# Hybrid encoder trunk on one core: phases in another order, the first 20 loads in a set order, two output projections 512 columns wide, transposes emitted ahead of attention

## The chip, the core and the metric

The kernel runs on one core of a Trainium2 chip. A core has TensorE (PE: matmuls and transposes, its weight loads shown as PEld), VectorE (DVE), ScalarE (ACT), GpSimd (POOL) and SyncE (SP, which here issues every DMA from one queue). Each engine takes its instructions in the order of the program and waits for the others by semaphores. The metric is the device time of one execution in microseconds, as the median of several runs.

## The reference

Two layers over a prompt `p` (1024 tokens) and a sample `s` (512 tokens) of width 1024, with the same weights. Each layer normalizes, projects once, runs three branches (even layer: gated short convolution, sliding-window attention, attention over 256 memory rows; odd layer: axial-rotary attention, differential attention, memory attention), gates with SiLU and projects back.

```python
def trunk(x, mem, norm_g, w_in, w_out, mem_norm_g, w_mem_kv, mem_qk_g, conv_w, swa_qk_g,
          swa_sink, ax_qk_g, diff_qk_g, diff_lambda, diff_subln_g):
...
    for l in range(DEPTH):
        h = rms_norm(x, norm_g[l])
        u = h @ w_in[l]
        mkv = rms_norm(mem, mem_norm_g[l]) @ w_mem_kv[l]
...
        if l % 2 == 0:
            y1 = short_conv(gb, gc, hc, conv_w[e])
            y2 = window_attention(q, k, heads(v, SWA_KV_HEADS), swa_sink[e])
        else:
            y1 = dense_gqa(q, k, heads(v, AX_KV_HEADS))
            y2 = diff_attention(dq, dk, heads(dv, DIFF_HEADS), diff_lambda[o], diff_subln_g[o], l)
        ym = memory_attention(mq, mk, mv)
        y = jnp.concatenate([y1, y2, ym], axis=-1)
        x = x + (y * jax.nn.silu(z)) @ w_out[l]
    return x
```

## The kernel before

**Arithmetic.** Matmuls run on fp32r numbers. So that no precision is lost, an operand is split in two: `hi` is its rounding (ACT casts), `lo` the rest (DVE or POOL subtracts, `split`, L198). A product takes three matmuls: hi x hi, hi x lo, lo x hi (L322 to L324, L336 to L338). Attention takes two (L596, L597).

**Phases.** `STEPS` is a list of phases, each a call of `step`: `in g l chunks` projects 512 or 1024 tokens onto 256-column chunks of `w_in` (`in_proj`, matmul tiles `pa`, `pb0`, `pb1`); `swa`, `ax`, `diff`, `mem` are the attentions (scores `s`, exponentials `e`, transposes `pT`, outputs `o`); `load` and `loady` fetch h or y from DRAM and split them (`alo`, `ahi`); `out g l half` is an output projection of 512 tokens (`out_proj`, tile `po`), which adds x (`xr`) and stores; `norm` normalizes rows for the next layer (transposes `hT`, products with the gain `hg`, `ht`). g is `p` or `s`, l the layer.

**An output projection** goes through four chunks of 256 columns. For each it loads five pieces of weights (`load_w`: `wraw`, 256 KB, split in `whi` and `wlo`), and for four tiles of 128 tokens it adds up 10 steps of 128 rows in one PSUM half bank, three matmuls of 128x256 each, so each piece is used by four tiles in turn. Two tiles share a bank, one VectorE addition empties it (L935).

**What sets the order.** The program is written phase by phase; a scheduler then orders each engine's instructions by priority and readiness. Attention phases are `urgent` (high priority), so their instructions are woven into the projections that are written after them. Small background steps (`BG`: norms, rope tables) and the pending transposes of projected heads (`TAIL`, `STACK`: `stT` with its source `raw`) are put in at `between` and `flush`, in the middle of a projection's matmuls. `ring` gives tiles out of a set number of buffers (`BUF_TABLE`: three `wraw`, seven `whi` and `wlo`, three `xh` for x, PSUM tags `s` 2, `t` 2, `d` 2, `x` 1, `o` 1 banks), and `in_order` keeps the first writes of a ring's tiles in the order in which they were asked for.

**The start.** Norm steps of the four memory tiles (`x`, `hT`, `hg`, `h0`, `h1`) come first, then the rope tables (`rope_table`, a POOL multiplication of 128x1024, L170), constants, the memory projection `mem_kv` (tile `pm`) and the norm of the first half of the prompt.

## Time and profile before

| | |
|---|---|
| time, median of 3 runs (lowest to highest) | 2108.88 us (2107.57 to 2109.26) |
| the profiled execution's own time | 2099.39 us |
| its span | 2097.6 us |
| mean granted TensorE clock over the span | 0.997 |
| busy: PE, DVE, ACT, POOL | 97%, 74%, 53%, 46% |

The span runs from the program's first instruction to its last. A stretch of the span is given by its start and end in us from the start. A matmul's duration is from its start to its modelled end; the next may start long before that end, so PE's throughput is read from the distance between starts, or from a count in a stretch. In a list of instructions, the bracket behind a row is the time for which the engine stood idle just ahead of it, and what ended that.

### The profile page before, as it was taken

What the parts mean: (1) busy time and instruction counts of PE and PEld (TensorE: products, weight loads), DVE (VectorE), ACT (ScalarE), POOL (GpSimd) and SP (SyncE); (2) the same over time, 40 slices, a digit from 0 to 9 for tenths busy, and PEclk for the clock granted to TensorE, in tenths of its full rate; (3) what the DMA queues carried; (4) which work ended last, traced back from release to release, by engine and by line L of the source; (5) the groups of instructions that cost most, each with busy time, mean ns of one, the idle gap of its engine ahead of it and who ended that gap; (6) DMA issues with size and microseconds to landing.
All of it is one profiled execution on the core that took longest, in us unless ns stands there. A gap on an engine that the chain in (4) does not pass through costs nothing.

```text
span 2097.6 us, 40483 instructions
## 1 busy us (share of the span) xinstructions
PE 2040.2 (97%) x14056; PEld 1885.0 (90%) x14056; DVE 1552.4 (74%) x3340; ACT 1115.9 (53%) x2634; POOL 969.9 (46%) x994
## 2 busy tenths in 40 slices
...
GB/s 236 206 241 197 228 106 91 118 101 217 238 236 224 209 93 82 104 154 128 82 151 154 226 164 178 151 199 213 169 218 199 160 191 193 157 235 225 233 159 106
DMA packets 323420, 365.79 MB, mean 174 GB/s; under 512 B 28048, under 2 KB 229520, under 8 KB 323216
## 3 DMA queue, kind: packets, MB, share of 16 engines
...
q14 instruction: 93, 0.76, 0.1%
...
## 4 chain that ended last, share of the span: by engine, by line
PE 75%; DMA 7%; DVE 7%; issue 3%; POOL 2%; ACT 1%; SPq 1%; DVEq 0%; POOLq 0%; ACTq 0%
PE pb L338 8%; PE pb L336 8%; PE pb L337 8%; PE pa L323 5%; PE pa L324 5%; PE pa L322 5%; PE po L322 4%; PE po L323 4%; PE po L324 4%; PE s L596 4%; PE s L597 4%; PE o L754 3%; PE pT L750 3%; PE o L685 1%; PE pT L683 1%
## 5 line engine op out<-in xcount | busy, mean ns | idle before, releaser
L200 POOL TENSOR_TENSOR wlo<-wraw,whi 128x512 fp32r<-128x512 f32 x182 | 249.0, 1370 | 329.1 <-ACT whi L199 309.9
L695 ACT ACTIVATE e<-s,nm 128x512 f32<-128x512 f32 (+1 forms) x416 | 265.1, 640 | 221.2 <-DVE nm L693 167.4
L199 ACT CAST whi<-wraw 128x512 fp32r<-128x512 f32 x388 | 236.9, 622 | 238.8 <-PE po L324 84.6
L604 DVE TENSOR_TENSOR ptlo<-pT,pthi 128x512 fp32r<-128x512 f32 x352 | 237.3, 683 | 41.6 <-ACT pthi L603 40.0
L693 DVE TENSOR_REDUCE nm<-s 128x1 f32<-128x512 f32 (+1 forms) x368 | 249.0, 682 | 25.7 <-PE s L597 24.4
L603 ACT CAST pthi<-pT 128x512 fp32r<-128x512 f32 x352 | 199.1, 588 | 114.6 <-PE pT L683 56.6
L322 PE MATMUL po<-whi,ahi 128*128 128x256 f32 x896 | 254.0, 284 | 0.4 <-DVE xr L935 0.4
L324 PE MATMUL po<-whi,alo 128*128 128x256 f32 x896 | 253.1, 284 | 1.3 <-DVE alo L200 1.3
L323 PE MATMUL po<-wlo,ahi 128*128 128x256 f32 x896 | 254.2, 284 | 0.0
L200 DVE TENSOR_TENSOR wlo<-wraw,whi 128x512 fp32r<-128x512 f32 x206 | 170.8, 830 | 95.3 <-ACT whi L199 92.5
L236 POOL TENSOR_TENSOR rs<-ss,mhalf 128x8 f32<-128x8 f32 (+2 forms) x108 | 141.1, 1307 | 174.4 <-DVE ss L232 125.2
L322 PE MATMUL pa<-whi,ahi 128*128 128x256 f32 x768 | 220.2, 287 | 0.5 <-ACT raw L394 0.4
L324 PE MATMUL pa<-whi,alo 128*128 128x256 f32 x768 | 219.2, 286 | 0.5 <-DVE alo L200 0.5
L323 PE MATMUL pa<-wlo,ahi 128*128 128x256 f32 x768 | 219.2, 285 | 0.0
L596 PE MATMUL s<-k,qhh 128*128 128x512 f32 (+2 forms) x512 | 190.1, 376 | 10.5 <-ACT e L695 9.6
L597 PE MATMUL s<-k,qll 128*128 128x512 f32 (+2 forms) x512 | 182.9, 363 | 2.8 <-DMA qll<-st_p1mq 1.6
L324 PEld LDWEIGHTS po<-whi,alo 128*128 128x128 f32 x896 | 171.0, 191 | 3.2 <-DVE alo L200 1.7
L322 PEld LDWEIGHTS po<-whi,ahi 128*128 128x128 f32 x896 | 171.1, 191 | 1.9 <-DVE xr L935 0.6
L323 PEld LDWEIGHTS po<-wlo,ahi 128*128 128x128 f32 x896 | 171.1, 191 | 1.2
L336 PE MATMUL pb<-h,whi 128*128 128x512 f32 x432 | 170.9, 396 | 0.0
L338 PE MATMUL pb<-h,wlo 128*128 128x512 f32 x432 | 170.7, 395 | 0.0
L337 PE MATMUL pb<-h,whi 128*128 128x512 f32 x432 | 170.6, 395 | 0.0
(170 smaller groups left out, 6022.7 us busy)
## 6 DMA issues: line engine op xcount, KB each, us to landing
wraw<-in_w_in_dram SPq DMA_DIRECT2D x252, 256.0 KB, 3.3
wraw<-in_w_out_dram SPq DMA_DIRECT2D x120, 256.0 KB, 3.2
...
zg_p<-z SPq DMA_DIRECT2D x32, 256.0 KB, 2.7
...
```

The source lines that it names most:

```text
L200: lo_eng.tensor_tensor(out=out_lo, in0=src, in1=f32(out_hi), op=ALU.subtract)
L322: nc.tensor.matmul(out=out, lhsT=h, rhs=wh, start=(k == 0), stop=False)
L323: nc.tensor.matmul(out=out, lhsT=h, rhs=wl, start=False, stop=False)
L324: nc.tensor.matmul(out=out, lhsT=l_, rhs=wh, start=False, stop=(k == n - 1))
L336: nc.tensor.matmul(out=out, lhsT=wh, rhs=h, start=(k == 0), stop=False)
L337: nc.tensor.matmul(out=out, lhsT=wh, rhs=l_, start=False, stop=False)
L338: nc.tensor.matmul(out=out, lhsT=wl, rhs=h, start=False, stop=(k == n - 1))
L596: nc.tensor.matmul(out=out, lhsT=q2[0], rhs=k, start=True, stop=False)
L597: nc.tensor.matmul(out=out, lhsT=q2[1], rhs=k, start=False, stop=True)
L604: nc.vector.tensor_tensor(out=lo, in0=ps, in1=f32(hi), op=ALU.subtract)
L693: nc.vector.tensor_reduce(out=nm, in_=s, axis=AXL.X, op=ALU.max, negate=True)
L695: nc.scalar.activation(out=e[:, j, :], in_=s[:, j, :], func=ACTF.Exp, bias=nm[:, j:j + 1], accum_out=su[:, j:j + 1],)
```

## The change

1. `STEPS`: the phases stand in another order at nine places (chunks moved between `in` steps, `diff p 1 0` ahead of `diff p 0 0`, `mem p 1 0` ahead of `diff p 2 0`, `mem s 1` behind `out p 1 0`, and others).
2. `load_w` now takes single steps of 128 rows, 512 columns of them: `w_out` lies in DRAM as 10 x 128 rows x 512 columns per half, and a narrow projection reads 256-column parts of it, two steps to a piece.
3. `out p 0 0` and `out s 1 0` become `outk`: `out_proj_k` goes through two chunks of 512 columns, holds four PSUM banks (two of tag `d`, two of `t`), one for each tile of 128 tokens, and for each of the 10 steps runs all four tiles, three matmuls of 128x512 each. Each of the four additions takes a whole bank.
4. At the start, 20 transposes of the identity; the first memory weights are asked for ahead of the rope tables and constants, which move behind the second x of the prompt; `ORDER` chains the first 20 loads (and the tiles that they write) in the order of the text.
5. `step` calls `flush` ahead of every attention phase, and `loady` calls `gate_now`, so pending transposes and gates are written ahead of it.

```diff
@@ -37,16 +37,16 @@
 CHUNKS = [L0_CHUNKS, L1_CHUNKS]
 STEPS = [
     "in p 0 kv0+q0+z4", "swa p 0", "in p 0 q1+z6+mq0", "swa p 1", "in p 0 z8", "mem p 0",
-    "in p 0 gch0+gbz0+gch1+gbz1+gch2+gbz2", "loady p 0 0 0 4", "in p 0 gch3+gbz3", "loady p 0 0 4 5",
-    "loady p 0 1", "out p 0 0", "norm p 0", "out p 0 1", "norm p 1", "load m", "load p 1 01", "memkv m",
-    "in p 1 kv0+q0+z0", "ax p 0", "in p 1 q1+z2+dk0+dv0", "ax p 1", "in p 1 dq0+z4", "diff p 0 1", "diff p 0 0",
-    "diff p 1 0", "in p 1 dq1+dv1", "in p 1 z6 0", "in p 1 dk1", "in p 1 mq0+z8 0", "load s 0 0",
-    "in s 0 kv0+q0+z4", "swa s 0", "in s 0 q1+z6", "swa s 1", "in s 0 mq0+z8", "mem s 0", "diff p 1 1",
-    "in s 0 gch0+gbz0+gch1+gbz1+gch2+gbz2+gch3", "load p 1 1", "in s 0 gbz3", "loady s 0 0 0 4", "in p 1 z6 1",
-    "diff p 2 0", "diff p 3 0", "mem p 1 0", "out s 0 0", "norm s", "in p 1 mq0+z8 1", "diff p 2 1", "diff p 3 1",
-    "in s 1 dv0", "mem p 1 1", "in s 1 kv0+q0+z0", "ax s 0", "in s 1 q1+dk0+z2+dq0", "ax s 1", "in s 1 z4",
-    "diff s 0", "diff s 1", "loady p 1 0", "in s 1 dk1+dq1+mq0+dv1+z8+z6", "diff s 2", "diff s 3", "mem s 1",
-    "loady p 1 1", "out p 1 0", "loady s 1 0 0 4", "out p 1 1", "out s 1 0",
+    "in p 0 gch0+gbz0+gch1+gbz1+gch2+gbz2+gch3", "loady p 0 0 0 4", "in p 0 gbz3", "loady p 0 0 4 5",
+    "loady p 0 1", "outk p 0 0", "norm p 0", "out p 0 1", "norm p 1", "load m", "load p 1 01", "memkv m",
+    "in p 1 kv0+q0+z0", "ax p 0", "in p 1 q1+dk0+dv0+z2", "ax p 1", "in p 1 dq0+z4", "diff p 1 0",
+    "in p 1 dq1+dv1", "diff p 0 0", "diff p 0 1", "in p 1 z6 0", "in p 1 dk1", "in p 1 mq0 0", "load s 0 0",
+    "in p 1 z8 0", "in s 0 kv0+q0+z4+q1", "swa s 0", "in s 0 z6", "swa s 1", "in s 0 mq0+z8", "mem s 0",
+    "diff p 1 1", "in s 0 gch0+gbz0+gch1+gbz1+gch2+gbz2+gch3", "load p 1 1", "in s 0 gbz3", "loady s 0 0 0 4",
+    "in p 1 z6 1", "mem p 1 0", "diff p 2 0", "diff p 3 0", "out s 0 0", "norm s", "in p 1 mq0+z8 1", "in s 1 dv0",
+    "diff p 2 1", "diff p 3 1", "in s 1 q0+kv0", "mem p 1 1", "in s 1 z0", "ax s 0", "in s 1 q1+dk0+z2+dq0",
+    "ax s 1", "in s 1 z4", "diff s 0", "diff s 1", "loady p 1 0", "in s 1 dk1+dq1+mq0+dv1+z8+z6", "diff s 2",
+    "diff s 3", "loady p 1 1", "out p 1 0", "loady s 1 0 0 4", "mem s 1", "out p 1 1", "outk s 1 0",
 ]
 BUF_TABLE = {
     "act": 16, "whi": 7, "wlo": 7, "wraw": 3, "xh": 3, "stk": 4, "bw": 5, "tb": 2, "sm": 12, "nm": 8, "sx": 6, "su": 12, "sk": 4, "s4": 2,
@@ -139,12 +139,21 @@
     lam_init = 0.8 - 0.6 * math.exp(-0.3 * 1)
     CW = const.tile([128, 4, 3], F32, name="convw_half")
 
+    ORDER = []
+
+    def loaded(t):
+
+        if len(ORDER) < 20:
+            ORDER.append(t)
+        return t
+
     def load_constants():
+        for t in (wmask, nsink, convw, gsub):
+            loaded(t)
         nc.sync.dma_start(out=wmask, in_=a["wmask"].rearrange("s p j -> p s j"))
         nc.sync.dma_start(out=nsink, in_=a["swa_sink"][0].partition_broadcast(128))
         nc.vector.tensor_scalar(out=nsink, in0=nsink, scalar1=-1.0, scalar2=None, op0=ALU.mult)
         nc.sync.dma_start(out=convw, in_=a["conv_w"])
-        nc.sync.dma_start(out=mg, in_=a["mem_qk_g"].partition_broadcast(128))
         nc.sync.dma_start(out=gsub, in_=a["diff_subln_g"].rearrange("o p -> p o"))
         nc.vector.tensor_scalar(out=gsub, in0=gsub, scalar1=0.5 * (1.0 - lam_init), scalar2=None, op0=ALU.mult)
         lv = tabt(4 * HD, "lv").rearrange("p (k d) -> p k d", k=4)
@@ -214,16 +223,20 @@
         return g
 
     @first
-    def load_w(src, pairs):
+    def load_w(src, ks, wide=False):
+
+
         hi, lo = [], []
-        for kp in pairs:
-            lo_ = ring(sb, [128, 2, 256], F32R, "wlo", "wlo")
-            h = ring(sb, [128, 2, 256], F32R, "whi", "whi")
-            raw = ring(sb, [128, 2, 256], F32, "wraw", "wraw")
-            dma(out=raw, in_=src[kp].rearrange("p (k n) -> p k n", k=2))
-            split(h, lo_, raw, nc.vector if kp % 2 == 0 else nc.gpsimd)
-            hi.append(h)
-            lo.append(lo_)
+        for k in ks:
+            l_ = ring(sb, [128, 512], F32R, "wlo", "wlo")
+            h = ring(sb, [128, 512], F32R, "whi", "whi")
+            raw = loaded(ring(sb, [128, 512], F32, "wraw", "wraw"))
+            dma(out=raw if len(src.shape) == 3 else raw.rearrange("p (i n) -> p i n", i=2), in_=src[k])
+            split(h, l_, raw, nc.vector if k % 2 == 0 else nc.gpsimd)
+            for i in range(1 if wide else 2):
+                sl = slice(0, 512) if wide else slice(256 * i, 256 * i + 256)
+                hi.append(h[:, sl])
+                lo.append(l_[:, sl])
         return hi, lo
 
     def rstd(out, ss, mul, add):
...
@@ -922,7 +935,9 @@
         for ci in range(4):
             if ahead and ci == 3:
                 ahead()
-            w = load_w(a["w_out"][l, ci], Y_ORDER[g, l])
+            w = load_w(
+                a["w_out"][l, ci // 2][:, :, ci % 2 * 256:ci % 2 * 256 + 256].rearrange("(k i) p n -> k p i n", i=2), Y_ORDER[g, l]
+            )
             for tp in range(2):
                 ps = ring(psum, [128, 2, 256], F32, "d", "po")
                 for t in range(2):
@@ -935,6 +950,37 @@
                 nc.vector.tensor_tensor(out=xr, in0=ps, in1=xr, op=ALU.add)
                 dma(out=dst[rows, cols].rearrange("(t p) n -> p t n", p=128), in_=xr)
 
+    def out_proj_k(g, l, hf, ys):
+
+
+        src = a[f"x_{g}"] if l == 0 else S[g, "x1"]
+        dst = S[g, "x1"] if l == 0 else a[f"out_{g}"]
+        order = [2 * kp + i for kp in Y_ORDER[g, l] for i in range(2)]
+        for ci in range(2):
+            cols = slice(ci * 512, (ci + 1) * 512)
+            rows = [slice(hf * 512 + t * 128, hf * 512 + (t + 1) * 128) for t in range(4)]
+            ps = [ring(psum, [128, 512], F32, "d", "pk") for _ in range(2)]
+            ps += [ring(psum, [128, 512], F32, "t", "pk", "A") for _ in range(2)]
+            xr = []
+            for n, k in enumerate(order):
+                (wh,), (wl,) = load_w(a["w_out"][l, ci], [k], True)
+                hi, lo = ys[n // 2]
+                for t in range(4):
+                    sl = slice(t * 128, (t + 1) * 128)
+                    h, l_ = hi[:, n % 2, sl], lo[:, n % 2, sl]
+                    nc.tensor.matmul(out=ps[t], lhsT=h, rhs=wh, start=(n == 0), stop=False)
+                    nc.tensor.matmul(out=ps[t], lhsT=h, rhs=wl, start=False, stop=False)
+                    nc.tensor.matmul(out=ps[t], lhsT=l_, rhs=wh, start=False, stop=(n == 9))
+                if n < 9:
+                    between(0)
+                if n >= 5 and n < 9:
+                    x = bw("xr")
+                    dma(out=x, in_=src[rows[n - 5], cols])
+                    xr.append(x)
+            for t in range(4):
+                nc.vector.tensor_tensor(out=xr[t], in0=ps[t], in1=xr[t], op=ALU.add)
+                dma(out=dst[rows[t], cols], in_=xr[t])
+
 
     nxt = {}
 
@@ -948,17 +994,23 @@
 
     hm, hp = new_h(), [new_h(), new_h()]
     gains = const.tile([128, 4, KT], F32, name="gains")
-    dma(out=gains, in_=a["gains"])
     g0, g1, gm0, gm1 = (gains[:, i, :] for i in range(4))
+    warm = ring(psum, [128, 4, 128], F32, "x", "warm")
+    for n in range(20):
+        nc.tensor.transpose(warm[:, n % 4, :], ident, ident)
     BG.extend(norm_steps(mem_rows(), put_act(hm, gm0), "s"))
-    bg(12)
+    bg()
+    dma(out=loaded(gains), in_=a["gains"])
+    w0 = load_w(a["w_mem_kv"][0, 0], range(2))
+    bg()
+    w1 = load_w(a["w_mem_kv"][0, 0], range(2, 4))
+    bg(10)
+    dma(out=loaded(mg), in_=a["mem_qk_g"].partition_broadcast(128))
     BG.extend(norm_steps(rows_of(a["x_p"]), put_act(hp[0], g0), "s"))
-    bg(3)
-    rope_table("swa_k", "e")
-    rope_table("swa_q", "e")
-    load_constants()
-    mem_kv(0, hm)
-    bg(12)
+    BG[2:2] = [lambda: rope_table("swa_k", "e")]
+    BG[4:4] = [lambda: rope_table("swa_q", "e"), load_constants]
+    mem_kv(0, hm, w0=tuple(x + y for x, y in zip(w0, w1)))
+    bg(len(BG))
     BG.extend(norm_steps(rows_of(a["x_p"], 1), put_act(hp[1], g0), "s"))
     BG.extend(norm_steps(rows_of(a["x_s"]), put_dram(S["s", 0, "h"], 0, g0)))
     BG.extend(norm_steps(mem_rows(), put_dram(S["m", 1, "h"], 0, gm1)))
@@ -972,14 +1024,16 @@
         flush()
 
     def step(op, g, *x):
+        if op in ("swa", "ax", "diff", "mem"):
+            flush()
         if op == "in":
             l = int(x[0])
             ids = [CHUNKS[l].index((c.rstrip("0123456789"), int(c.lstrip("abcdefghijklmnopqrstuvwxyz")))) for c in x[1].split("+")]
             in_proj(g, l, H[g, l], ids, hfs=[int(h) for h in x[2]] if len(x) > 2 else None)
         elif op == "swa":
-            swa(g, int(x[0]))
+            swa(g, *map(int, x))
         elif op == "ax":
-            ax(g, int(x[0]))
+            ax(g, *map(int, x))
         elif op == "diff":
             diff(g, int(x[0]), int(x[1]) if len(x) > 1 else None)
         elif op == "mem":
...
                 H[g, l] = [load_half(g, l, hf) if hf in hfs else None for hf in range(GROUPS[g] // 512)]
         elif op == "loady":
+            gate_now()
             settle()
             l, hf = int(x[0]), int(x[1])
             part = slice(int(x[2]), int(x[3])) if len(x) > 2 else slice(0, 5)
             YS.setdefault((g, l, hf), []).extend(load_y(g, l, hf, part))
@@ -1070,7 +1126,7 @@
     out["mem_s"] = f["mem_sample"][0]
     out["w_in"] = np.stack([np.stack([pieces(f["w_in"][l], cols(l, *c)) for c in CHUNKS[l]]) for l in range(2)])
     out["w_out"] = np.stack(
-        [np.stack([pieces(f["w_out"][l], np.arange(256 * c, 256 * c + 256)) for c in range(4)]) for l in range(2)])
+        [f["w_out"][l].reshape(10, 128, 2, 512).transpose(2, 0, 1, 3) for l in range(2)])
     out["w_mem_kv"] = np.stack(
         [np.stack([pieces(f["w_mem_kv"][l], np.arange(256 * c, 256 * c + 256)) for c in range(2)]) for l in range(2)])
     out["conv_w"] = f["conv_w"][0].reshape(3, 4, 128).transpose(2, 1, 0)

```

Three places show what this does to the engines' own orders.

SP, the first DMAs of the program. `x` are tiles of 128 tokens to be normalized, `wraw` weights, `cs` and `g` a rope table's parts. Before:

```order
L119 DMA x<-in_mem_p_dram 128x1024 x2
L119 DMA x<-in_mem_s_dram 128x1024
L119 DMA gains<-in_gains_dram 128x32
L167 DMA g_300<-in_rope_g_dram 128x128
L169 DMA cs<-in_rope_dram 128x1024
L167 DMA g_307<-in_rope_g_dram 128x128
L169 DMA cs<-in_rope_dram 128x1024
L143 DMA wmask<-in_wmask_dram 128x2x128
L144 DMA nsink<-in_swa_sink_dram 128x8
L146 DMA convw<-in_conv_w_dram 128x12
L147 DMA mg<-in_mem_qk_g_dram 128x256
L148 DMA gsub<-in_diff_subln_g_dram 128x1
```

And with the change:

```order
L119 DMA x<-in_mem_p_dram 128x1024
L157 DMA gsub<-in_diff_subln_g_dram 128x1
L119 DMA gains<-in_gains_dram 128x32
L119 DMA wraw<-in_w_mem_kv_dram 128x512 x2
L119 DMA x<-in_mem_p_dram 128x1024
L119 DMA wraw<-in_w_mem_kv_dram 128x512 x2
L119 DMA x<-in_mem_s_dram 128x1024
L119 DMA wraw<-in_w_mem_kv_dram 128x512
L119 DMA x<-in_mem_s_dram 128x1024
L119 DMA mg<-in_mem_qk_g_dram 128x256
L119 DMA wraw<-in_w_mem_kv_dram 128x512 x2
```

The weights of the memory projection, behind all of the rows shown before, now alternate with the x; rope tables and the other constants come later.

PE, inside `out p 0 0`, with buffer numbers; the first operand's halves are `whi`, `wlo`, the second's `ahi`, `alo`. Before:

```order
L322 MATMUL po_6157<-whi_6063,ahi_5713 128x256
L323 MATMUL po_6157<-wlo_6062,ahi_5713 128x256
L324 MATMUL po_6157<-whi_6063,alo_5712 128x256
L322 MATMUL po_6157<-whi_6063,ahi_5713 128x256
L323 MATMUL po_6157<-wlo_6062,ahi_5713 128x256
L324 MATMUL po_6157<-whi_6063,alo_5712 128x256
L322 MATMUL po_6157<-whi_6069,ahi_5720 128x256
```

And with the change:

```order
L971 MATMUL pk_6083<-whi_6238,ahi_6042 128x512
L972 MATMUL pk_6083<-wlo_6237,ahi_6042 128x512
L973 MATMUL pk_6083<-whi_6238,alo_6041 128x512
L971 MATMUL pk_6084<-whi_6238,ahi_6042 128x512
L972 MATMUL pk_6084<-wlo_6237,ahi_6042 128x512
L973 MATMUL pk_6084<-whi_6238,alo_6041 128x512
L971 MATMUL pk_6085<-whi_6238,ahi_6042 128x512
L972 MATMUL pk_6085<-wlo_6237,ahi_6042 128x512
L973 MATMUL pk_6085<-whi_6238,alo_6041 128x512
L971 MATMUL pk_6086<-whi_6238,ahi_6042 128x512
```

One piece of weights now serves four accumulators in a row, at twice the columns, where before one accumulator went through all pieces.

VectorE, at the end of `out p 0 0` and the beginning of `out p 0 1`. `alo` is the split of y (`alo_6041` to `alo_6055` before, `alo_6048` to `alo_6076` after belong to the second half of y), `xr` an addition that empties a bank, `wlo` a weight's split, `ss`, `x` and `ht` the norm. Before:

```order
L935 TENSOR_TENSOR xr_6698<-po_6637,xr_6698 128x512
L259 TENSOR_SCALAR x_6702<-x_6702,rs_6707 128x1024
L232 TENSOR_SCALAR ss_6714<-ss_6714 128x1
L259 TENSOR_SCALAR x_6711<-x_6711,rs_6716 128x1024
L200 TENSOR_TENSOR alo_6048<-alo_6048,ahi_6049 128x512 x2
L200 TENSOR_TENSOR wlo_6922<-wraw_6924,whi_6923 128x512
L277 TENSOR_TENSOR ht_6774<-hT_6769,gains_139 128x512
L200 TENSOR_TENSOR alo_6055<-alo_6055,ahi_6056 128x512
L277 TENSOR_TENSOR ht_6812<-hT_6807,gains_139 128x512
L200 TENSOR_TENSOR alo_6055<-alo_6055,ahi_6056 128x512
L277 TENSOR_TENSOR ht_6894<-hT_6889,gains_139 128x512
```

And with the change:

```order
L209 TENSOR_TENSOR alo_6069<-alo_6069,ahi_6070 128x512 x2
L209 TENSOR_TENSOR wlo_6510<-wraw_6512,whi_6511 128x512
L209 TENSOR_TENSOR alo_6076<-alo_6076,ahi_6077 128x512 x2
L209 TENSOR_TENSOR wlo_6522<-wraw_6524,whi_6523 128x512
L209 TENSOR_TENSOR alo_7323<-alo_7323,ahi_7324 128x512 x2
L209 TENSOR_TENSOR wlo_6528<-wraw_6530,whi_6529 128x512
L209 TENSOR_TENSOR alo_7330<-alo_7330,ahi_7331 128x512
L981 TENSOR_TENSOR xr_6395<-pk_6283,xr_6395 128x512
L209 TENSOR_TENSOR alo_7330<-alo_7330,ahi_7331 128x512
L981 TENSOR_TENSOR xr_6415<-pk_6284,xr_6415 128x512
L209 TENSOR_TENSOR wlo_6703<-wraw_6705,whi_6704 128x512
L981 TENSOR_TENSOR xr_6435<-pk_6285,xr_6435 128x512
```

The last splits of y moved from behind the last addition to ahead of the last four; two splits of h for the memory (`alo_7323`, `alo_7330`) stand there now.

## Rows read from the trace of the kernel before

**Rows 1.** The page, part 1: busy us (share of the span), instructions.
```profile
PE 2040.2 (97%) x14056; PEld 1885.0 (90%) x14056; DVE 1552.4 (74%) x3340; ACT 1115.9 (53%) x2634; POOL 969.9 (46%) x994
```
**Rows 2.** Stretches: length, busy us of each engine, clock, DMA share, GB/s.
```profile
0.00:26.00 26.00, 12.00 (x51) 10.61 (x52) 18.65 (x28) 11.62 (x23) 15.19 (x19) 1.00 0.79 263
1200.00:1600.00 400.00, 390.56 (x2455) 349.02 (x2454) 337.08 (x777) 235.84 (x591) 177.31 (x182) 0.99 0.63 189
```
**Rows 3.** Chain that ended last: start us, us on the chain, what.
```profile
500.12 0.12 PE po L323
...
111.42 0.23 PE pb L336
```
**Rows 4.** Stretches inside `out p 0 0` and inside an `in p 0` phase.
```profile
500.00:540.00 40.00, 40.00 (x336) 40.00 (x335) 12.70 (x19) 10.98 (x19) 7.34 (x7) 1.00 0.63 200
476.00:492.00 16.00, 16.00 (x72) 13.24 (x71) 9.17 (x16) 5.47 (x10) 1.30 (x1) 1.00 0.63 201
```
**Rows 5.** Groups by shape (count | busy us, mean ns), 493 to 551, last 1440 to 1680.
```profile
L200 DVE TENSOR_TENSOR wlo<-wraw,whi 128x512 fp32r<-128x512 f32 x13 | 8.9, 690 | 18.1 <-ACT whi L199 17.9
...
L199 ACT CAST whi<-wraw 128x512 fp32r<-128x512 f32 x19 | 11.6, 619 | 32.7 <-PE po L324 21.9 <-DMA wraw<-in_w_out_dram 10.2
...
L200 DVE TENSOR_TENSOR wlo<-wraw,whi 128x512 fp32r<-128x512 f32 x25 | 19.7, 788 | 4.4 <-ACT whi L199 4.0
```
**Rows 6.** DMA issues: count, KB each, median us from issue to landing.
```profile
wraw<-in_w_out_dram SPq DMA_DIRECT2D x120, 256.0 KB, 3.2
...
xr<-in_x_p_dram SPq DMA_DIRECT2D x16, 256.0 KB, 5.7
```
**Rows 7.** Instructions of the start: start us, us, engine, line [idle before].
```profile
4.46 1.06 ACT L256 ACTIVATE sqx<-x 128x1024 bf16<-128x1024 f32 x1 [2.46 <-DMA x<-in_mem_p_dram]
...
5.71 1.06 ACT L256 ACTIVATE sqx<-x 128x1024 bf16<-128x1024 f32 x1
...
9.84 1.97 PE L266 MATMUL hT<-ident_r,x 128*128 128x128 f32 x8 [0.57 <-DVE hg L277]
10.84 2.40 POOL L170 TENSOR_TENSOR cs<-cs,g 128x1024 f32<-128x1024 f32 x1 [1.41 <-DMA cs<-in_rope_dram]
10.96 3.43 DVE L292 TENSOR_TENSOR h<-hg,h 128x256 fp32r<-128x256 f32 x2
...
14.29 1.26 ACT L199 CAST whi<-wraw 128x512 fp32r<-128x512 f32 x2 [3.15 <-DMA wraw<-in_w_mem_kv_dram]
...
17.89 0.58 PE L323 MATMUL pm<-wlo,h 128*128 128x256 f32 x1 [2.34 <-DVE wlo L200]
...
40.59 1.11 PE L266 MATMUL hT<-ident_r,x 128*128 128x128 f32 x4 [3.28 <-DVE hg L277]
...
55.54 0.28 PE L322 MATMUL pa<-whi,h 128*128 128x256 f32 x1
```
**Rows 8.** Stretches of the start.
```profile
18.00:26.20 8.20, 7.56 (x34) 7.27 (x35) 8.01 (x11) 3.71 (x10) 5.64 (x6) 1.00 0.75 295
26.20:36.00 9.80, 9.80 (x84) 9.80 (x84) 8.53 (x16) 8.37 (x19) 6.61 (x8) 1.00 0.76 236
...
39.00:44.00 5.00, 3.41 (x19) 3.41 (x20) 4.87 (x10) 3.45 (x10) 3.52 (x5) 0.66 0.65 213
```
**Rows 9.** PE instructions that waited, at `out p 0 1` and at `memkv m`.
```profile
557.10 0.39 PE L324 MATMUL po<-whi,alo 128*128 128x256 f32 x1 [0.58 <-DVE alo L200]
...
570.94 0.39 PE L322 MATMUL po<-whi,ahi 128*128 128x256 f32 x1 [0.37 <-DVE xr L935]
...
632.40 0.66 PE L266 MATMUL hT<-ident_r,x 128*128 128x128 f32 x4 [1.69 <-DVE ss L232]
```
**Rows 10.** Stretches in the middle, between attentions of the second layer.
```profile
1166.00:1206.00 40.00, 34.13 (x262) 32.26 (x261) 39.42 (x93) 26.11 (x67) 21.35 (x22) 1.00 0.74 228
1560.00:1600.00 40.00, 34.44 (x190) 29.04 (x189) 34.51 (x70) 25.84 (x58) 20.00 (x18) 0.91 0.74 222
1500.00:1680.00 180.00, 170.25 (x1205) 156.97 (x1203) 155.75 (x348) 114.45 (x294) 98.84 (x103) 0.98 0.63 187
```

27 lines of the change are left out of this document (14 added, 13 removed).

## The prediction

> **What bounds the kernel now.** I read the page first. TensorE (PE) is busy 2040.2 us, 97% of the span of 2097.6 [rows 1]. So the time can only fall in two ways: cheaper matmuls, or less of the 57.4 us in which PE idles. The second view says where it idles: PE's busy time beside a stretch's length. The first 26 us lose 14.0; of four stretches of 400 us from 400 to 2000, the worst, from 1200 on, loses 9.4 [rows 2].
>
> What a matmul costs is not its mean duration, since matmuls overlap. In the chain that ended last, where PE waits for nothing, a 256-column one follows the last after 0.12 us and a 512-column one after 0.23 [rows 3]. By counts, 336 of 256 columns stand in 40 us and 72 of 512 in 16 us [rows 4]. A window also counts some two matmuls that only reach into it, so I use 40/334 = 0.120 and 16/70.3 = 0.228 us.
>
> **Two projections with 512 columns.** Before, one projection of 512 tokens is 4 x 2 x 2 x 10 x 3 = 480 matmuls of 256 columns, 57.6 us. Now it is 2 x 10 x 4 x 3 = 240 of 512, 54.7. That is 2.9 each, **5.8 us** for the two. It lies on the path: from 500 to 540 us, inside the first of them, PE is busy 40.00 of 40 [rows 4]. What could take it back is weights and banks. A piece of weights (256 KB either way) now feeds 12 matmuls, 2.7 us; before, five pieces feed 120, 2.9 each. ACT's cast of one takes 0.62 and VectorE's subtraction 0.69 [rows 5], so neither is near its limit. The four accumulators end 3 matmuls, 0.68 us, apart; an addition is of the size of that subtraction, 0.69, and the first bank is asked for again 9 matmuls, 2.05 us, after its last one. I cost that at nothing; where a split of 0.69 stands ahead of the addition it can cost up to 0.7. At the very end four stores follow each other instead of one: I add 0.5 (0 to 1).
>
> The Trainium skill, page "TensorE: Matmul & The Clock Gate", section "Wait — 56ns, not 53.3ns?", has a smaller gain: there a warm matmul starts N / 2.4 GHz plus about 2.5 ns after the one ahead of it, so half as many save 2.7 ns per pair, an estimate of 1.3 us for both projections in place of 5.8. The rows here give 12 ns per pair [rows 4].
>
> The other, narrow projections read the weights' new layout in half as long pieces, 1 KB as the loads of `xr` do. Those land after 5.7 us (256 KB), the present weights after 3.2 [rows 6]. Between bounds of 0 and 2.5 us per load I take 0 on the path: the waits of PE at a projection are for `alo`, `hT` and `xr` [rows 9], none for a weight.
>
> **The start.** Before, three x, the gains, two rope tables and five constants are issued ahead of the first weight. ACT waits 3.15 us for it, until 14.29, and PE has its second matmul of the memory projection at 17.89 [rows 7]. VectorE is held too: two `h` take it 3.43 us beside a rope table that POOL multiplies for 2.40 [rows 7].
>
> In the new order two weights stand right behind the first x and the gains. The first x still lands at 4.46. 512 KB take 1.25 us (the second square starts at 5.71 [rows 7]), so the second x, behind two weights, lands near 7.4, the third, behind two more that wait for a buffer, at about 10.9. VectorE's queue decides, as its new order goes: x·rs of the second x (square 1.06 + 0.19 on ACT, rs on POOL behind a split, 0.75) ends near 10.8; two `hg` 12.1; then it waits for the cast of the fifth weight, which stands behind the third square on ACT (12.2 + 0.62); its subtraction 13.5; `h` 14.0. So PE works steadily from about **14.0 instead of 17.9**. From there it has 28.5 us of work up to the first matmul of `in p 0`, at 55.54 before [rows 7], 9.1 lost on the way. Of that, 3.28 is one wait at 40.59 [rows 7], with a granted clock of 0.66 around it [rows 8], 1.4 more; about 4 is the low level: from 18 to 26.2 us PE has 34 instructions, in the next 9.8 us 84 [rows 8], that is 0.21 us between matmuls against 0.12, 1.2 GHz against 2.4. In the new order each of those transposes stands 3 us of PE work or more behind what releases it, where that one has 0.4, so I drop the wait and its clock (4.7) and keep the 4. The two rope multiplications (2.4 us each) now fall inside this stretch and hold VectorE, so I give back 1.6. That brings the first `in p 0` matmul to about 48.5, **7 us** earlier. Bounds: VectorE fully in the way and the rope tables later than their readers, +1; the high clock from the first weight on, -12.
>
> The 20 transposes on the identity cost nothing by themselves, as PE is idle there. Before, transposes until 11.8 us [rows 7], with a gap behind them, were not enough: the spacing falls to 0.12 only at 26.2 [rows 8], 8 us after the last long wait. The new 20 have the same gap behind them, up to the first x. The Trainium skill, same page, section "Part 1: The HAM clock gate (the "warmup" mystery)", calls the throttled state the default, which activity releases: by that the 20 could lift the clock ahead of the first projection, 4 us more. The rows here speak for the gap.
>
> **The second half of y and the norm.** From 557 to 571 us PE waits four times, 0.58 first and 0.37 last [rows 9], 3.0 in all against the spacing of 0.12. VectorE splits the second half of y (`alo`) late there, and the norm's transposes follow each other by 1.2 to 1.8 us of PE work. In the new order the splits of y stand ahead of the wide projection's last additions, and the transposes 3 us or more apart. I take **-2.5** (0 to -3). The waits at 630 and 632 us, 1.69 at the latter [rows 9], have the same neighbours as before and stay.
>
> **The reordered phases.** In the middle, waits bunch where VectorE can't keep up: from 1166 to 1206 us it is busy 39.42 of 40 and PE 34.13; from 1560 to 1600 PE has 34.44 at a granted clock of 0.91 [rows 10]. I set each VectorE instruction, at the median time of its kind, beside the PE work that its place in the order covers. Per 40 us of PE work, from 1080 us of it on (1126 in the trace), before has 0.94 and 1.18, after 1.08 and 1.05; from 1440 on (1500 in the trace), before has 0.92, 0.84, 1.17, 1.01, after 1.00, 1.00, 1.13, 1.02. What lies over 1 is 14.4 us before and 11.2 after: spread, not removed. So the moved phases are worth **-2**. The ends: -10, the bunched waits of one place gone, and +10, the 8.4 us more VectorE work in the second place all lost and one more stretch at the low clock. The transposes emitted ahead of attention keep their distance of 5.4 us of PE work (median, in both) from what they wait for, so I give them nothing of their own.
>
> **Sum.** -5.8 - 7 - 2.5 - 2 + 0.5 = -16.8. The profiled execution took 2099.4 with its span of 2097.6, 9.5 under the median of 2108.9; I carry the difference over to the median: **2092 us**, beside a span of about 2081.
>
> **Rivals.**
> *Only the projections pay.* VectorE sets the start whatever is loaded first, and the moves cost what they give: -5.8, 2103 (2099 to 2104.6). For it: VectorE is near its limit at both places [rows 10]. Against: at the start part of its time is held up, not work [rows 7].
> *The waits in the middle dissolve*: 10 more, 2081.
> *The clock comes early*, by activity: 2088.
> *The wide matmul gains only 1.3* if each costs its columns and little else: 2096.
> *Nothing*: start +1, moves +8, and the projections' gain: 2107.
> *Slower, by VectorE* from 1440 us of PE work on. Its load is 1.0 or more for 160 us of PE work, 166 us at median times, without a slack piece ahead. But its instructions run over the median there: `wlo` 788 ns in that stretch against 690 beside a projection [rows 5], and all kinds together 11%. At 15% its 191 us beside 160 leave 31, where PE idles 9.8 now (1500 to 1680 us [rows 10]); two more stretches at the low clock cost 3.4. With the other terms that is -14.8 + 21 + 3.4 = +10, 2118. It decides from about 12% on. Against: before also runs 11% over there, and PE idles less than that surplus, as it runs ahead by its buffers.
>
> **How the numbers follow.** Forecast (2085 to 2099) 0.41; early clock 0.09; small wide gain 0.06; middle dissolves 0.12; only the projections 0.18; nothing 0.08; slower 0.06. The likeliest is 2092. Under 2104.7 (0.2%, about what a measurement of this kernel tells from no change) lie the first five: 0.86 faster, 0.08 same, 0.06 slower. The range from 2080 to 2106 leaves out half of the best case, most of "nothing", and the slower one.
>
> **What would show it.** Right: wide matmuls 0.228 us apart, and 54.7 us for each of the two projections; the memory projection's second matmul before 15 us, the first matmul of `in p 0` before 50; no wait of PE over 0.5 us from 550 to 575. Wrong: that first matmul after 53 us; a wait for a bank longer than 0.7 us in a wide projection; or, between 1500 and 1680 us, PE idle for over 15 us.

## The result and the profile after

The changed kernel takes **2119.8 us** (median of 6 runs, 2113.3 to 2124.1), the kernel before 2107.7 beside it: a ratio of 1.0057 (95%: 1.0038 to 1.0075), 12 us slower. The profiled execution of after took 2121.5 with a span of 2119.7 and stands at its median; that of before [rows 1] lies 8 under its own. So the two traces differ by 22 us where the kernels differ by 12, and before is read below from several kernels that share its order. One execution of the experiments, the profiled one of the kernel before with x by rs on ACT, took 3836 us at a mean clock of 0.883 and is left out.

The page of after, part 1, answers to [rows 1]:

```profile
PE 2051.0 (97%) x13596; PEld 1869.9 (88%) x13596; DVE 1550.8 (73%) x3336; ACT 1114.6 (53%) x2634; POOL 976.7 (46%) x998
```

There are 460 fewer matmuls and transposes, and PE is busy 11 us longer; it idles 68.7 us, 57.4 before. The two wide projections run as forecast. A stretch inside the first, one in the last, and a row of the chain that ended last (two matmuls there take 0.45):

```profile
508.00:548.00 40.00, 40.00 (x178) 33.14 (x177) 16.03 (x22) 14.87 (x26) 12.66 (x10) 1.00 0.72 241
2070.00:2110.00 40.00, 40.00 (x177) 33.01 (x176) 6.23 (x9) 6.33 (x11) 7.71 (x6) 1.00 0.37 112
...
2102.48 0.45 PE pk L973 x2
```

That is 40/176 = 0.227 us per matmul, 54.5 for each projection, with no wait for a bank. The first matmul of `in p 0`, too, comes as forecast, 7.2 us earlier than in [rows 7]; PE's rows there:

```profile
1.61 4.43 PE L1000 MATMUL warm<-ident_r 128*128 128x128 f32 x20 [1.61 <-DVE ident_r L128]
8.92 1.73 PE L279 MATMUL hT<-ident_r,x 128*128 128x128 f32 x8 [2.88 <-DVE x L272]
12.66 1.97 PE L279 MATMUL hT<-ident_r,x 128*128 128x128 f32 x8 [2.01 <-DVE hg L290]
...
15.23 0.42 PE L336 MATMUL pm<-wlo,h 128*128 128x256 f32 x1
...
48.37 0.35 PE L335 MATMUL pa<-whi,h 128*128 128x256 f32 x1
```

The loss stands behind it. Three stretches of the first 260 us, of before and then of after (length, busy us of PE, PEld, DVE, ACT, POOL, clock, DMA share, GB/s):

```profile
0.00:60.00 60.00, 42.72 (x298) 41.10 (x299) 48.53 (x79) 35.94 (x79) 41.77 (x45) 0.97 0.71 226
60.00:160.00 100.00, 99.26 (x736) 94.17 (x734) 76.70 (x164) 46.17 (x110) 58.61 (x63) 1.00 0.77 229
160.00:260.00 100.00, 97.08 (x615) 86.96 (x614) 88.45 (x216) 49.57 (x120) 44.38 (x34) 1.00 0.74 211
```
```profile
0.00:60.00 60.00, 48.75 (x352) 46.38 (x353) 46.19 (x79) 36.03 (x78) 43.34 (x45) 0.91 0.74 236
60.00:160.00 100.00, 90.94 (x636) 84.64 (x635) 67.37 (x142) 41.15 (x101) 51.95 (x56) 0.97 0.73 212
160.00:260.00 100.00, 93.19 (x597) 83.76 (x596) 89.69 (x201) 47.54 (x113) 50.54 (x40) 0.97 0.68 197
```

PE has 54 instructions more behind it at 60 us, 20 of them the transposes of the identity, but from 60 to 160 it gets through 636 instead of 736. VectorE has not come forward at all: 79 instructions by 60 us in both, and 142 against 164 in the next 100. It is not full there: 67.37 us of 100, and 89.69 in the 100 behind. The longest waits of PE behind the first matmul of `in p 0` (start, us, [idle before]):

```profile
50.41 0.63 PE L279 MATMUL hT<-ident_r,x 128*128 128x128 f32 x4 [1.69 <-DVE x L272]
67.55 0.58 PE L335 MATMUL pa<-whi,h 128*128 128x256 f32 x1 [2.43 <-ACT raw L407]
...
123.68 0.63 PE L388 MATMUL stT<-ident_r,raw 128*128 128x128 f32 x4 [2.06 <-DVE raw L441]
125.64 0.77 PE L609 MATMUL s<-k,qhh 128*128 128x256 f32 x2 [1.33 <-DMA qhh<-st_p0q]
149.85 0.50 PE L698 MATMUL o<-pthi,v 128*128 128x512 f32 x1 [1.70 <-ACT pthi L616]
225.06 0.66 PE L279 MATMUL hT<-ident_r,x 128*128 128x128 f32 x4 [1.00 <-DVE ht L290]
235.52 0.44 PE L609 MATMUL s<-k,qhh 128*128 128x384 f32 x1 [1.31 <-ACT e L681]
241.38 1.08 PE L388 MATMUL stT<-ident_r,raw 128*128 128x128 f32 x4 [2.38 <-DVE su L685]
```

Before has one wait over 1 us in this stretch, 2.2 at 232. Three of after's draw the clock down as well (means of three stretches):

```profile
60.00:70.00 10.00, 7.57 (x54) 7.25 (x53) 6.92 (x15) 5.64 (x17) 3.38 (x6) 0.86 0.52 168
120.00:130.00 10.00, 6.60 (x27) 5.08 (x26) 6.98 (x11) 1.80 (x3) 5.10 (x5) 0.83 0.79 234
240.00:250.00 10.00, 7.63 (x42) 7.37 (x42) 9.52 (x23) 3.92 (x10) 5.94 (x5) 0.66 0.79 248
```

The wait at 67.55 is not for VectorE. PE waits there for ACT's copy out of a bank, which stands behind a square (ACT, L269) that waits for a load of x; VectorE, too, is idle until that square is done:

```profile
66.09 1.06 ACT L269 ACTIVATE sqx<-x 128x1024 bf16<-128x1024 f32 x1 [1.75 <-DMA x<-in_x_p_dram]
...
67.14 0.35 ACT L407 COPY raw<-pa 128x256 f32<-128x256 f32 x1
```
```profile
67.27 0.15 DVE L245 TENSOR_SCALAR ss<-ss 128x1 f32<-128x1 f32 x1 [2.45 <-ACT sqx L269]
```

At the third place of the prediction, the second half of y, the waits of [rows 9] from 557 to 571 us are gone, and two others stand 20 us later, at the next projection's banks:

```profile
550.00:575.00 25.00, 25.00 (x155) 22.31 (x154) 11.59 (x19) 9.15 (x16) 4.42 (x4) 1.00 0.80 254
```
```profile
580.93 0.36 PE L335 MATMUL po<-whi,ahi 128*128 128x256 f32 x1 [1.37 <-DVE xr L950]
...
591.84 0.39 PE L335 MATMUL po<-whi,ahi 128*128 128x256 f32 x1 [2.61 <-DVE xr L950]
```

At the fourth place PE idles as much as in [rows 10], 10.1 us against 9.8, but VectorE is busy 162.4 us instead of 155.8:

```profile
1500.00:1680.00 180.00, 169.93 (x1208) 155.86 (x1207) 162.39 (x376) 115.38 (x285) 92.88 (x87) 1.00 0.59 176
```

To compare kernels whose clocks have slipped against each other, I count PE's **own work**: every matmul or transpose at its spacing without waits (0.109 us for a transpose, 0.120, 0.175 and 0.228 for 256, 384 and 512 columns). What a trace takes beyond it is lost, and can be told by own work done. One profile each, up to PE's last instruction:

| us lost between (us of own work) | 0, 40 | 40, 400 | 520, 640 | 640, 1440 | 1440, 1720 | 1720, end |
|---|---|---|---|---|---|---|
| before | 25.1 | 6.1 | 9.1 | 18.8 | 20.0 | 6.8 |
| after | 18.9 | 26.0 | 12.9 | 18.8 | 24.8 | 10.4 |

Own work is 5.8 less in after for the wide projections, and 2.2 more for the 20 transposes of the identity, which stand in its first 40 us and are no work of before's. Counting only work that both kernels have, after loses 21.2 there, and its lead is 4.0 us at 40 us of work (61.2 against 65.2). At 60 us the lead is gone (86.1 against 85.9); at 400 after is 16.0 us behind (447.2 against 431.2).

### The profile page after: what moved, and what is told of

Read it like the earlier page. It is cut to its first block, busy times and chain, and to the rows that moved or that the text cites. A ratio compares the mean times of both kernels' runs of the same rounds, so it can differ in the third digit from the quotient of the medians.

```text
span 2119.7 us, 39555 instructions
## 1 busy us (share of the span) xinstructions
PE 2051.0 (97%) x13596; PEld 1869.9 (88%) x13596; DVE 1550.8 (73%) x3336; ACT 1114.6 (53%) x2634; POOL 976.7 (46%) x998
## 5 line engine op out<-in xcount | busy, mean ns | idle before, releaser
L209 DVE TENSOR_TENSOR wlo<-wraw,whi 128x512 fp32r<-128x512 f32 x202 | 164.1, 813 | 117.7 <-ACT whi L208 116.3
L335 PE MATMUL po<-whi,ahi 128*128 128x256 f32 x608 | 173.7, 286 | 4.0 <-DVE xr L950 4.0
L337 PE MATMUL po<-whi,alo 128*128 128x256 f32 x608 | 173.9, 286 | 0.3 <-DVE alo L209 0.3
L336 PE MATMUL po<-wlo,ahi 128*128 128x256 f32 x608 | 172.9, 285 | 0.0
L335 PE MATMUL pa<-whi,h 128*128 128x256 f32 x576 | 166.7, 290 | 2.4 <-ACT raw L407 2.4
L337 PE MATMUL pa<-whi,h 128*128 128x256 f32 x576 | 167.0, 290 | 0.6 <-DVE h L305 0.6
L336 PE MATMUL pa<-wlo,h 128*128 128x256 f32 x576 | 167.0, 290 | 0.5 <-POOL wlo L209 0.5
```

Of the source, the lines that this page charges most:

```text
L209: lo_eng.tensor_tensor(out=out_lo, in0=src, in1=f32(out_hi), op=ALU.subtract)
L335: nc.tensor.matmul(out=out, lhsT=h, rhs=wh, start=(k == 0), stop=False)
L336: nc.tensor.matmul(out=out, lhsT=h, rhs=wl, start=False, stop=False)
L337: nc.tensor.matmul(out=out, lhsT=l_, rhs=wh, start=False, stop=(k == n - 1))
```

## The experiments

All times are medians; the intervals are of the ratio to before, which ran beside each. A microsecond difference of two kernels is good to about 3 (before) or 5 (two others).

**One part of the change undone.** First, `flush()` ahead of attention:

```diff
-        if op in ("swa", "ax", "diff", "mem"):
-            flush()
```


> The changed kernel without the transposes emitted ahead of attention: pending transposes wait again until the next projection comes past. In the changed kernel TensorE loses 25.5 us between 80 and 280 us of its own work, 5.5 before; two of the waits there, 2.22 us at 123.7 and 2.54 at 241.4, are transposes of q and mq heads just ahead of attention on heads that VectorE has just made. Theory A (these transposes stand too near to what they wait for, and every attention pays): about 2104, the 20 us are back down to 6 or so. Theory B (the new start pushes VectorE's and the queue's work into 60 to 250 us): 2118 to 2120. Theory C (the moved phases): 2118 to 2120. Theory D (any change redraws the order everywhere and the loss has no single cause): anything from 2108 to 2125, with other waits than in the changed kernel.

2118.4, 1.0045 (1.0030 to 1.0060): 1.4 less than after, no difference that can be told. Theory A falls; PE's emitted order is that of after up to 400 us of own work, and 23.8 us are lost from 40 to 400.

The start (lines of before back in place of the new ones, and no `chains["loads", ""]`):

```diff
-    warm = ring(psum, [128, 4, 128], F32, "x", "warm")
...
-    BG[2:2] = [lambda: rope_table("swa_k", "e")]
-    BG[4:4] = [lambda: rope_table("swa_q", "e"), load_constants]
-    mem_kv(0, hm, w0=tuple(x + y for x, y in zip(w0, w1)))
...
+    rope_table("swa_k", "e")
+    rope_table("swa_q", "e")
+    load_constants()
+    mem_kv(0, hm)
...
```


> The changed kernel with the start of before: no transposes on the identity, loads in the order in which the scheduler places them, rope tables and constants ahead of the memory projection. Theory B (the start shifts work into 60 to 250 us): the 20 us there are back, the 6 us gained in the first 60 us go, so about 2106. Theory A (transposes ahead of attention) and theory C (moved phases): the 6 us of the start go and nothing comes back, 2126. Theory D: 2108 to 2125.

2108.8, 1.0006 (0.9992 to 1.0019): **11 us of the loss are the new start's.** Up to 400 us of own work its emitted order of PE is before's, row for row, and behind 480 after's; it loses 26.4 us up to 40 and 5.8 from 40 to 400. Its stretch answers to the second one above:

```profile
60.00:160.00 100.00, 99.06 (x734) 93.89 (x733) 75.65 (x159) 44.40 (x105) 59.43 (x64) 1.00 0.77 228
```

The phases in the order of before (`STEPS`, with the two `outk` kept):

> The changed kernel with the phases in the order of before (the two wide projections stay). Theory C (the moved phases cost what is lost): 2105 or below. By the two traces the moved places stand at 1080 to 1240 us of TensorE's own work, where it loses 12.9 against 14.5 before, at 1440 to 1680, 24.8 against 19.5, and at 1760 to 1840, 6.9 against 5, so theories A and B give 2114 to 2119, the 5 us of the last two back at most. Theory D: 2108 to 2125.

2114.5, 1.0030 (1.0014 to 1.0046): 5.4 less than after. From 1440 to 1720 it loses 18.6, after 24.8; behind that 6.3 against 10.4.

The wide projections narrow again (`outk` to `out`):

> The changed kernel with the two wide projections in 256 columns again (the weights' layout stays). If half as many matmuls of twice the columns gain 2.9 us for each of the two, as their spacing of 0.227 us in the changed kernel says: 2125.6. If the gain is lost again elsewhere, or was no gain: 2119 to 2121. Theory D: anything from 2110 to 2135, with waits at other places.

2120.0, 1.0058 (1.0036 to 1.0079): the same as after. Its own work is 5.7 longer, but from 520 to 640 it loses 8.8 where after loses 12.9. Nothing of the gain shows in the time.

**One part alone, or part of the start.** The bound order of the loads taken away, the rest of the start kept:

```diff
-    chains["loads", ""] = ORDER
```


> The changed kernel with all of its new start but without the bound order of the first 20 loads. Without that chain the emitted order of TensorE's work from 80 to 400 us of it agrees with the kernel before in 88 to 98 of 100 rows, with it in 17 to 87. Theory B1 (the chain is what redraws that order, and the redrawn order costs 16 us there): the 6 us gained in the first 60 us stay, 80 to 280 us of TensorE's own work lose about 5 as before and not 19.6, so about 2105. Theory B2 (the rope tables and constants among the norm steps, or the transposes on the identity, push work there): the 19.6 stay, 2118 to 2120.

2116.1, 1.0038 (1.0024 to 1.0053). Theory B1 falls: without the chain the loads go back to an order in which PE waits 10 us for the second `hT` (at 18.6), 26.2 us are lost up to 40 of own work, so the start's gain is gone; and 11.0 are still lost from 40 to 400.

The same start on the kernel before:

> The kernel before with the new start alone, without the chain: transposes on the identity, first two pieces of weights behind the first x, rope tables and constants among the norm steps; phases, attention and projections as before (the output weights lie in the new layout). Theory B1: start -6 as in the changed kernel, nothing lost behind it: about 2101. Theory B2: -6 + 14 = 2115. If half as long pieces of the weights cost the narrow projections something, more waits for weights in them, and up to 3 us more.

2113.1, 1.0031 (1.0020 to 1.0042): +7, as 24.4 up to 40 and 13.6 from 40 to 400. The start without the chain costs 7 by itself, and brings nothing. (It holds the 20 transposes, the early weights and the new places of the rope tables and constants; they were not tried one by one.) Both kernels without the chain have one emitted order of PE up to 400 us of own work, and it is before's in 95 of 100 rows from 40 to 400; they lose 5 to 7.5 us more than before there.

Both wide projections alone, and the last alone (`outk` in place of `out`):

> The kernel before with the two wide projections alone. The 5.8 us of fewer matmuls all arrive: 2101.4. Theory W (a wide projection ends its four row blocks together, so the norm's loads and the additions of the next projection crowd behind it, as the bank waits of 1.54 and 2.77 us at 580.9 and 591.8 in the changed kernel suggest): 4 us are given back behind the first one, 2105 to 2107, with waits for a bank behind an addition there.

> The kernel before with only the last projection wide, behind which nothing follows. By the spacing of 0.228 us: -2.9 and the stores at the end +0.5, so 2104.8. Theory W: the same 2104.8, and so faster than or level with both wide, though it has half of their gain. If a wide projection gains nothing by itself: 2107.

2104.4, 0.9991 (0.9978 to 1.0004), and 2108.0, 0.9994 (0.9979 to 1.0009). Neither can be told from before. The full 5.8 lies outside the first interval (-4.6 to +0.8), the 2.9 inside the second (-4.4 to +1.9). The second kernel's other projections read the weights' new layout in narrow pieces, so this costs nothing that shows either (a load lands after 3.4 us, 3.2 before). Behind the first wide projection there are waits again:

```profile
565.62 0.35 PE L336 MATMUL po<-whi,ahi 128*128 128x256 f32 x1 [1.13 <-DVE xr L951]
576.93 0.38 PE L336 MATMUL po<-whi,ahi 128*128 128x256 f32 x1 [3.02 <-DVE xr L951]
```

Beyond the spacing their pair measures 3.7 to 4.8 in the five profiles with a wide first projection that I read there; with a narrow one, the waits for a bank come to 0.5 to 2.1 in four. All that is lost from 520 to 640 of own work sums to 9.9 to 14.9 with the wide one and 8.8 to 13.0 with the narrow one (norms on VectorE): some 2 more, with much overlap. Theory W is right in kind; its 4 us are rather 2.

The moved phases alone:

> The kernel before with the moved phases alone (and the pending gates taken ahead of the loads of y, without which the new order would read what is not yet written). By the difference between the changed kernel and the one with the phases of before: +5.4, 2112.5. By the sum of the prediction: -2, 2105. If VectorE's load from 1440 us of TensorE's own work on is what costs, the loss stands between 1440 and 1680 there.

2109.7, 1.0015 (1.0001 to 1.0029): +2.4, between the two expectations. From 640 to 1440 nothing is gained over the kernels with old phases (16.7 here; those have 16.4 to 24.6), from 1440 to 1720 it loses 21.3. Over all profiles with norms on VectorE the old phases lose 18.6 to 21.3 there (6 kernels), the new ones 21.3 to 25.8 (8).

**Is it VectorE?** At 40 us of own work, reached at 65.2 us in before, 59.0 in after, and 64.5 in the kernel before with the new start unbound, VectorE's busy time is the fourth number (rows of the three kernels in this order):

```profile
0.00:65.20 65.20, 47.92 (x343) 46.30 (x344) 53.66 (x87) 38.50 (x86) 44.27 (x47) 0.97 0.72 228
```
```profile
0.00:59.00 59.00, 47.75 (x343) 45.38 (x344) 45.76 (x78) 35.13 (x77) 42.83 (x44) 0.91 0.74 233
```
```profile
0.00:64.50 64.50, 47.44 (x343) 45.48 (x344) 50.77 (x83) 36.09 (x82) 43.12 (x46) 0.84 0.67 222
```

PE has 343 instructions behind it in each; VectorE lacks 7.9 us in after, 2.9 in the third. From 40 to 400 they lose 6.1, 26.0 and 13.6. But 20 of the 343 are the transposes of the identity in the last two. At 40 us of the work that all three have, the rows of after and of the third are these:

```profile
0.00:61.17 61.17, 49.92 (x361) 47.55 (x362) 47.21 (x82) 36.54 (x80) 43.58 (x46) 0.92 0.74 238
```
```profile
0.00:66.67 66.67, 49.61 (x361) 47.65 (x362) 52.94 (x87) 37.09 (x84) 44.84 (x48) 0.85 0.68 224
```

So VectorE lacks 6.5 us (5 instructions) in after, and 0.7 (none) in the third, which loses 7.5 more than before all the same. VectorE's lag can't be the whole of it. To test this debt (theory V), the norm's multiplication of a tile of x by its value per row, rs, went to ACT, in after and in before:

```diff
-            nc.vector.tensor_scalar(out=x, in0=x, scalar1=rs, scalar2=None, op0=ALU.mult)
+            nc.scalar.activation(out=x, in_=x, func=ACTF.Copy, scale=rs)
```


> The changed kernel with the multiplication x by rs of every norm on ACT instead of VectorE. In the first 260 us that takes 20 instructions and 21.5 us off VectorE. Theory V (the start brought TensorE 6 us forward but not VectorE: when TensorE has done 40 us of its own work, VectorE has done 45.7 us against 53.7 before, and this debt is paid between 100 and 250 us with waits, low clock and round trips): the 20 to 26 us that TensorE loses from 40 to 400 us of its own work fall to 10 or less, about 2107. Theory O (the redrawn order alone, whatever VectorE's load): the loss there stays over 15, 2114 to 2120.

> The kernel before with the multiplication x by rs of every norm on ACT instead of VectorE, the control to the same edit of the changed kernel. TensorE loses 6 us from 40 to 400 us of its own work there, so at most 4 of these can come back, and some of the 25 of the first 40 us: 2100 to 2107 by either theory. If this gains as much as in the changed kernel, VectorE's load is a general bound and not what the change made worse.

2101.5, 0.9967 (0.9951 to 0.9982), **18 us less than after and 6 less than before**; but 2111.4, 1.0013 (1.0001 to 1.0025), on before. So it is no general bound. From 40 to 400 the changed kernel now loses 12.2. (Of the control there is so no profile to read.)

The other way, later norms instead of cheaper ones:

```diff
-    BG.extend(norm_steps(rows_of(a["x_s"]), put_dram(S["s", 0, "h"], 0, g0)))
-    BG.extend(norm_steps(mem_rows(), put_dram(S["m", 1, "h"], 0, gm1)))
...
+        if s == "swa p 1":
+            BG.extend(norm_steps(rows_of(a["x_s"]), put_dram(S["s", 0, "h"], 0, g0)))
+            BG.extend(norm_steps(mem_rows(), put_dram(S["m", 1, "h"], 0, gm1)))
```


> The changed kernel with the norms of the sample's rows and of the second layer's memory rows (8 tiles of x, 8 multiplications by rs and 16 by the gains, about 20 us of VectorE) put behind the second window attention instead of among the first projections. Theory V: VectorE's debt can be paid in the space that this makes, the 20 to 26 us lost from 40 to 400 us of TensorE's own work fall to 10 or less, about 2107. Theory O: over 15 stay, 2114 or more. If the norms crowd where they now stand, new waits on hT and ht between 250 and 480.

> The kernel before with the same norms put behind the second window attention, the control. It loses 6 us from 40 to 400 of TensorE's own work, most of it the wait for an attention's product at 232: at most 4 come back, 2102 to 2107.

2124.4, 1.0078 (1.0060 to 1.0097), and 2110.8, 1.0017 (1.0005 to 1.0030): a miss, in both. From 100 of own work on, hardly anything is lost any more in either (1.3 us up to 400), as theory V has it; but 17.8 and 7.0 are lost from 80 to 100, ahead of the first attention. With the norms gone, the rope tables of later phases came forward to there. Rows of PE, ACT and POOL in the changed kernel with late norms:

```profile
118.51 1.08 PE L388 MATMUL stT<-ident_r,raw 128*128 128x128 f32 x4 [4.23 <-DVE raw L441]
```
```profile
114.65 0.62 ACT L208 CAST whi<-wraw 128x512 fp32r<-128x512 f32 x1 [5.68 <-DMA wraw<-in_w_in_dram]
```
```profile
112.37 2.38 POOL L179 TENSOR_TENSOR cs<-cs,g 128x1024 f32<-128x1024 f32 x1
...
123.39 1.41 POOL L434 TENSOR_TENSOR sq<-raw,tb 128x256 f32<-128x256 f32 x2 [5.75 <-DMA tb<-tab_swa_q]
```

POOL multiplies a later table (`cs`) between the steps that make q, the loads that ACT and POOL wait for stand behind the tables' loads and stores in SP's queue, and the first attention starts at 132 instead of 125.6.

**The same parts with x by rs on ACT.** Three kernels: the changed one with the old start; with the old phases, no `flush()` and no `gate_now`; and before with the wide projections.

> The changed kernel with x by rs on ACT, and with the start of before. Theory V (VectorE's debt is why the new start costs 11 us; with less load on VectorE the new start gains what it moves TensorE forward): slower than the changed kernel with x by rs on ACT (2101.45), by some 4 to 7, 2105 to 2109. Theory O (it is only chance of the redrawn order): no sign is expected, 2095 to 2110. If the start is worse whatever VectorE's load: 2090 to 2096.

> The changed kernel with x by rs on ACT, with the new start and the wide projections, but phases and attention as before. If the moved phases cost their 5 us here too (with the phases of before the changed kernel gains 5.4): 2096. If they cost nothing once VectorE has less to do: 2100 to 2103.

> The kernel before with x by rs on ACT and the two wide projections, with start, phases and attention as before. By the sum of the two single edits (+3.8 and -1.8 against before): 2109.5. Against the run with the new start beside it, theory V has the new start ahead by 4 or more; theory O has no sign.

2099.7 (0.9967, 0.9953 to 0.9981), 2114.7 (1.0036, 1.0020 to 1.0052), 2112.4 (1.0021, 1.0007 to 1.0035). The new start now costs 1.8 and 2.3 in the two pairs, within the error: no longer 11, and not the gain of 4 or more that theory V expected. The phases are the surprise: with ACT's x the new ones (with `flush()`) are **13 us faster** than the old ones, in both pairs, where they were 2 to 5 slower.

**Where does ACT's x pay?** Only the first 20 tiles, in the changed kernel; and only the later norms, with the start of before. The first has PE's emitted order of the changed kernel with all x on ACT up to 480 us of own work, and that of the changed kernel behind it; the second that of the kernel with the old start, and behind 480 us that of the same with all x on ACT. `early` is true for the norms that are written ahead of the first phase.

```diff
+            if early:       # the other kernel: not early
+                nc.scalar.activation(out=x, in_=x, func=ACTF.Copy, scale=rs)
+            else:
+                nc.vector.tensor_scalar(out=x, in0=x, scalar1=rs, scalar2=None, op0=ALU.mult)
```


> The changed kernel with x by rs on ACT for the first 20 tiles of x alone, those of the first 260 us; behind 480 us of TensorE's own work its emitted order is that of the changed kernel, row for row. Theory V (VectorE's debt of the new start is paid between 40 and 400 us): the 26 us lost there fall to about 12, so 2106, with the rest as in the changed kernel. If the gain of 18 came from the later norms: 2117 to 2120.

> The changed kernel with the start of before and with x by rs on ACT for the later norms alone (of the first layer's sum and of the sample). Against the same kernel with all on VectorE (2108.8) and all on ACT (2099.67). If the moved phases pay only where the sample's norm comes in between 1440 and 1680 us of TensorE's own work with its x made by ACT: 2100 to 2102, and 7 us less lost in that stretch. If the 20 tiles at the start brought it: 2107 to 2109.

2107.8, 1.0005 (0.9992 to 1.0017): 12 us of the 18 stand at the start. With the old start the same 20 tiles on ACT change nothing (2098.9 without, 2099.7 with them). And 2098.9, 0.9968 (0.9955 to 0.9982): 10 us against the same kernel with VectorE's x, and the best version here, 0.32% faster than before. Two stretches of the first, to set beside those of after; then 1520 to 1700 with VectorE's x and with ACT's in the later norms:

```profile
60.00:160.00 100.00, 93.72 (x672) 88.03 (x671) 65.55 (x152) 50.15 (x112) 52.26 (x57) 0.98 0.74 219
160.00:260.00 100.00, 97.06 (x623) 87.34 (x622) 86.03 (x206) 53.30 (x124) 48.73 (x39) 1.00 0.72 204
```
```profile
1520.00:1700.00 180.00, 168.73 (x1193) 155.06 (x1192) 159.85 (x370) 114.31 (x297) 101.14 (x104) 0.99 0.62 184
```
```profile
1520.00:1700.00 180.00, 171.00 (x1232) 158.27 (x1231) 157.72 (x370) 118.55 (x304) 101.81 (x106) 1.00 0.63 189
```

The kernels together, one profile each:

| us lost between (us of own work) | 0, 40 | 40, 400 | 1440, 1720 | time |
|---|---|---|---|---|
| old start, VectorE's x, norms in their place (6 kernels) | 24.3 to 26.4 | 5.0 to 7.7 | | |
| old start, ACT's x (2) | 25.3, 26.6 | 7.5, 7.7 | | |
| new start, VectorE's x (4 kernels) | 18.7 to 19.5 | 20.9 to 26.0 | | |
| new start, ACT's x (3) | 18.3 to 18.9 | 10.8 to 13.7 | | |
| old phases, ACT's x late (2) | | | 25.8, 29.4 | 2112.4, 2114.7 |
| new phases, ACT's x late (3) | | | 17.3 to 19.1 | 2098.9 to 2101.5 |

The six kernels of the first row have one emitted order of PE up to 400 us of own work, the four of the third another. So the spread inside a row from 40 to 400 (2.7 and 5.1 us) is what single executions of one order differ by, and the 13 us between the rows are not.

## Why the prediction was wrong

I forecast 2092 (2080 to 2106); it took 2119.8.

*The projections, -5.8.* Spacing (0.227) and length (54.5) were right. Of the gain the time shows -1.8 on before (interval -4.6 to +0.8) and nothing on after. The Trainium skill, page "TensorE: Matmul & The Clock Gate", section "Wait — 56ns, not 53.3ns?", would have it at 1.2 by its 2.5 ns per matmul, an estimate (the prediction's 2.7 ns and 1.3 are a little high); the rows of after have 0.227 against 2 x 0.120 and contradict it for these matmuls, though the time, which has the new waits behind the first projection in it, can't tell the two.

*The second half of y, -2.5.* The waits named did go, but I put nothing in their place. Two waits for a bank of 1.37 and 2.61 us took it, both ended by an addition on VectorE. That the norm's work, which crowds behind the wide projection, held these additions up is argued from their place and not tested. The term was some 2 to 4 us off, with the wrong sign.

*The start, -7.* **This is the step that failed, in what I made of it.** The place was right: the first matmul of `in p 0` came at 48.37 (forecast 48.5), in part by luck. I had read 1.25 us for 512 KB from the second square at 5.71 [rows 7], but that one stood behind the first on ACT (1.06 + 0.19) and tells of no landing. The squares of the second and third x came at 8.96 and 12.30 (I had landings at 7.4 and 10.9), and the second `pm` at 15.23, not 14.0. Against that, the low level cost PE 2.1 us from there, not 4, and eight transposes (0.9 us) of the norm now stand behind that matmul instead of ahead of it.

I then carried these 7 us to the end of the kernel as if all behind them would move along. In the "start" paragraph I worked out VectorE's queue up to 14 us and stopped; that VectorE has the same work to do before the first attention, and does it no sooner, I held only against the start itself, in the rival "only the projections pay", with a chance of 0.18 and a cost of nothing. In fact a lead of 4.0 us in common work was left at 40 us of it and none at 60, and PE paid 20 us more than before between 40 and 400: the lead turned into 16 us lost in the traces, 11 in the times. VectorE, at the same work of PE, was 6.5 us behind. With 21.5 us off VectorE there, 12 come back, and with the old start none do.

What is shown: the new start costs 11, and nearly all of that cost goes when the 20 multiplications leave VectorE. What is not: that load alone is the cause. Without the chain VectorE has no lag and 5 to 7.5 us more are lost than before; the wait at which the lead went (2.43 at 67.55) hung on a late load of x, with VectorE idle; and in after VectorE is busy for 67 of the 100 us from 60 to 160 (but for 90 of the next 100). The order of the loads in SP's queue, as a cause of its own, was not tried. Each edit also redraws the order in which the scheduler emits that stretch, and no edit was found that changes the load and keeps the order.

*The reordered phases, -2 (-10 to +10).* +2.4 alone, 5.4 when undone from after, lost from 1440 of own work on, where the prediction had counted 8.4 us more VectorE work as the upper end. Inside the bounds, with the wrong sign: the middle that I took was not the row nearest to it. The rival "slower, by VectorE" gave 2118, close to the time, but not by its mechanism: PE idles 10.1 us from 1500 to 1680, not 31. That the same phases are 13 faster with ACT's x, and that ACT's x costs 4 to 8 with the old phases and the old start, stays open: VectorE loses 2 us of work in that stretch, too little to explain it, and the emitted order there is new.

*The transposes ahead of attention, nothing.* Right: 1.4, within the error.

*The 20 transposes.* There was the gap behind them, as I said, and the high clock was not there for the first projection (rival "early clock", 0.09). But the low level ended at 19.4, 4.2 us after the second `pm`, where before it lasted 8.4, so half of the 4 us that I kept did go. No run tells whether the transposes have a part in that.

The list of what would show it came out right at nearly every point (48.37, 0.227, 54.5, PE 25.00 of 25 from 550 to 575, idle 10.1 from 1500 to 1680; the second `pm` at 15.23, not before 15). It asked at the places that I had changed, and at none where the gain could be lost again. The rival "nothing" is added up wrongly: with its +1, +8, -5.8 and the -2.5 and +0.5 that it leaves as they were, it gives 2110, not 2107. The experiments do not add up exactly: undone alone, start, phases, `flush()` and projections give 11.0, 5.4, 1.4 and -0.2 of 12.
